# One product of the dense layers moved to the last place but one, and reads of banks and head statistics put ahead of weight splits

## The chip, the cores and the metric

The kernel runs on one core of a Trainium2 chip. Its engines are the matrix engine (PE, with PEld for its weight loads), the vector engine (DVE), the scalar engine (ACT), GpSimd (POOL) and SyncE (SP), which here only issues transfers. The metric is the device time of one execution in microseconds, as the median of several runs. Before the change it is 1388.97 us (three runs, 1386.44 to 1390.92).

## The reference

Two pre-norm residual layers over 512 tokens of width 1024, in float32, each a token mixer and a dense squared-ReLU block, and a final norm.

```python
def chunked_spatial_gating(xn, w_in, b_in, v_norm_g, w_s, b_s, w_out):   # mixer of layer 0
    u, v = split(gelu(xn @ w_in + b_in)); v = rmsnorm(v, v_norm_g)
    s = causal mix of v over chunks of 128 tokens by w_s, plus b_s
    return (u * s) @ w_out

def retention(xn, w_in, head_norm_g, w_out):                             # mixer of layer 1
    q, k, v, g = split(xn @ w_in)          # 4 heads, 256 for q and k, 512 for v and g
    o = decayed causal attention of rotary(q), rotary(k), v
    o = rmsnorm(o, head_norm_g) per head * silu(g)
    return o @ w_out

def squared_relu_mlp(h, w1, w2):                                         # 1024 -> 4096 -> 1024
    a = relu(h @ w1)
    return (a * a) @ w2

for i in range(2):
    x = x + mixer_i(rmsnorm(x, norm_mix_g[i]))
    x = x + squared_relu_mlp(rmsnorm(x, norm_ffn_g[i]), mlp_w1[i], mlp_w2[i])
return rmsnorm(x, final_norm_g)
```

## The kernel before, in words

**Splits.** Every float32 operand of a matmul is split into a high part, a cast to fp32r on ACT, and a low part, the operand less its high part, on DVE. A product is then three matmuls (`mm3`): high by high, high by low, low by high. Weights come in 1 MB tiles ("raw", one DMA each on SP's queue). A tile is used as two pieces; a piece gets its high part `wH` at L220 and its low part `wL` at L227.

**Order.** The kernel is a list of steps, written out by hand, and each engine works its instructions off in the order in which the steps emit them. A step is one piece of weights (24 matmuls for an up step or an output step, 12 for half a product of the kind below). Within a step `advance()` emits the next part of pending work (evacuations, activations), and `refill()` emits the weight work ahead: the casts up to the third piece after the step's own place, the low parts one piece less far. When all pieces of a tile are split, its slot is free and the next load is emitted; loads are emitted in the order of first use.

**The dense layers.** The up product makes 4096 features, 1024 at a time (`up` steps, eight pieces to a quarter). The down product of the first three quarters (q = 0, 1, 2: I call them thirds) is done by `seven`, a scheme with seven block products in place of eight: activations are kept as two blocks of features by two halves of tokens, and each of the products s = 0 to 6 multiplies one block, or a sum of blocks, with one weight block or a sum of weight blocks. `make(s)` forms and splits the activations of a product (sums on DVE at L748 to L755, cast at L763, low part at L764). Sums of weights are formed in memory: a second DMA, on POOL's queue (L199), adds a block onto the tile. The products 1, 3 and 6 share one tile: 3's weights are made by adding a block onto 1's once both pieces of 1 are split, 6's by adding onto 3's.

Each product accumulates into one of three pairs of PSUM banks, `BANK = "acbacaa"` by s, named smLQa, smLQb and smLQc in the profile (L the layer, Q the third); the bank of 0, 1 and 2 is opened there and later products add to what it holds. At the end of a product its bank is read into the token-major sum `ytok` or `xtok` (two instructions on DVE at L792, in the third 0 also on ACT). In the third 2 the steps stand as `upupupupuupuupp`: u is an up step, p a product, so that the last two products follow each other directly. After the last quarter's activations are ready, `split_a` splits them (L713, L714) for the last down product.

**The head statistics.** In layer 1, `o_unit` multiplies one head's gated output with its rows of the output weights, in four pieces (`ro`), and during it the norm of the next head is made by the generator `head_norm`: the sum of squares is split (ACT L316, POOL L317), summed over partitions by two matmuls (`st_h`, L325 and L326), scaled and put through a reciprocal square root on DVE (L329 to L303), split and laid on a diagonal (`dg_h`, L340), and spread over partitions by two matmuls (`bc_h`, L344 and L345). `out_piece` runs one piece: for each of two halves twelve matmuls, and in the second half `advance()`, `refill()` and then what the caller passes as `behind`.

Of the kernel before, what the change touches and what calls it, by code (L numbers as in the profile page):

```python
# [88 lines left out]
def trunk(ctx, tc, x, norm_mix_g, norm_ffn_g, a_w_in, a_b_in, a_v_norm_g, a_w_s, a_b_s, a_w_out,  # L89
# [16 lines left out]
    def tmp(name, tag, bufs=2):  # L106
        return work.tile([P, T], F32, tag=tag, name=name, bufs=bufs)
# [99 lines left out]
    def prep(upto, low=None):  # L207

        low = upto if low is None else low
        while pos["piece"] < min(upto, len(order)):  # L210
            p = order[pos["piece"]]
            if p.over is not None:
                lower(order.index(p.over) + 1)
            while any(raws.index(r) >= pos["raw"] for r in p.raws):
                load_raws()
                if any(raws.index(r) >= pos["raw"] for r in p.raws):
                    lower(pos["low"] + 1)
            prep_tiles(pos["piece"])
            p.src = p.make() if p.make else p.raws[0].tile[p.view]
            nc.scalar.copy(out=p.hi, in_=p.src)  # L220
            pos["piece"] += 1
        lower(low)
# [14 lines left out]
    def advance():  # L237
        for g in list(pending):
            if next(g, "end") == "end":
                pending.remove(g)  # L240
# [5 lines left out]
    def refill():  # L246
        n = pos["done"]
        prep(n + (LOOK if n >= 4 else 1), n + (LOOK - 1 if n >= 4 else 1))

    def step(fn, *ps):  # L250
        for p in ps:
            order.append(p)
            raws.extend(r for r in p.raws if r not in raws)
            for r in p.raws:
                r.uses += 1
        steps.append((fn, ps))
# [104 lines left out]
    def mm_o(p, t, ps, bH, bL):  # L361
        ts = slice(t * P, (t + 1) * P)
        for k in range(4):
            mm3(ps, p.hi[:, k, ts], p.lo[:, k, ts], bH[:, k, :], bL[:, k, :], k == 0, k == 3)
# [187 lines left out]
    def evac_x(gcol=None, scaled=False):  # L552

        def ev(i, ps):
            if scaled:
                t = tmp(f"xs{i}", "uz")
                nc.vector.tensor_mul(t, ps, r2bc)
                nc.vector.tensor_add(xT[i], xT[i], t)
            else:
                nc.vector.tensor_add(xT[i], xT[i], ps)  # L560
            if gcol is not None:
                norm_chunk(i, gcol)
        return ev

    def out_piece(p, i, h, name, gcol=None, before=None, behind=None, act=None, bank=acc, scaled=False):

        ev = evac_x(gcol, scaled)
        hi, lo = act or (yH, yL)

        def run(p):  # L570
            if before:
                before()
            for t in range(2):
                ps = bank(f"{name}{h}_{i}{t}")
                mm_o(p, t, ps, hi[h], lo[h])
                if t == 1:
                    advance()
                    refill()
                    if behind:
                        behind()  # L580
                ev(2 * i + t, ps)
        step(run, p)

    def nxt(g, times=1):
        return lambda: [next(g, None) for _ in range(times)]
# [133 lines left out]
    def seven(l, q):  # L719

        w = mlp_w2[l]

        def part(i, j):
            r, c = 1024 * q + 512 * i, 512 * j
            return w[r : r + 512, c : c + 512].rearrange("(k p) n -> p k n", p=P)

        t1 = Raw(part(0, 0), adds=[part(0, 1)])
        t2 = Raw(part(1, 1), adds=[part(1, 1)], over=t1)
        t4 = Raw(part(1, 0), adds=[part(1, 0)], over=t2)
        wraws = [Raw(part(0, 0)), t1, Raw(part(1, 0)), t2, Raw(part(1, 1)), Raw(part(0, 1), adds=[part(1, 1)]), t4]  # L730
        pl = [[Piece(r, (slice(None), slice(2 * i, 2 * i + 2), slice(None)), [P, 2, 512]) for i in range(2)] for r in wraws]
        lo_t, hi_t = slice(0, T // 2), slice(T // 2, T)
        sums, parts, banks = {}, {}, {}

        def block(h, ts, c):
            return aF[2 * q + h][:, 2 * c : 2 * c + 2, ts]

        def half(v):
            return v.rearrange("p (k t) -> p k t", t=T // 2)

        def make(s):

            def src(c):
                if s in (0, 2, 6):
                    return block(*((0, lo_t), None, (1, lo_t), None, None, None, (1, hi_t))[s], c)
                if s == 1:
                    sums["s", c] = half(tmp(f"sa{l}{q}{c}", "uz"))
                    nc.vector.tensor_sub(out=sums["s", c], in0=block(0, hi_t, c), in1=block(1, hi_t, c))  # L748
                elif s == 3:
                    nc.vector.tensor_sub(out=sums["s", c], in0=sums["s", c], in1=block(0, lo_t, c))  # L750
                elif s == 4:
                    nc.vector.tensor_add(out=sums["s", c], in0=sums["s", c], in1=block(1, lo_t, c))
                else:
                    sums["d", c] = half(tmp(f"sd{l}{q}{c}", "sq"))
                    nc.vector.tensor_sub(out=sums["d", c], in0=block(0, lo_t, c), in1=block(0, hi_t, c))  # L755
                    return sums["d", c]
                return sums["s", c]

            sp = parts[s] = big([P, 2, 4, T // 2], F32R, f"sp{l}{q}{s}")
            for c in range(2):  # L760
                v = src(c)
                hi, lo = sp[:, 0, 2 * c : 2 * c + 2, :], sp[:, 1, 2 * c : 2 * c + 2, :]
                nc.scalar.copy(out=hi, in_=v)  # L763
                nc.vector.tensor_sub(out=lo, in0=v, in1=f32(hi))  # L764

        BANK = "acbacaa"
        FIRST = (0, 1, 2)
        OUT = [((0, 0), ALU.add), ((1, 1), ALU.add), ((0, 0), ALU.add), ((0, 1), ALU.subtract), ((0, 1), ALU.add), ((1, 1), ALU.subtract), ((1, 0), ALU.add)]

        def one(s, i):  # L770
            def run(p):
                bk = BANK[s]
                if i == 0 and s in FIRST:
                    banks[bk] = [acc(f"sm{l}{q}{bk}{t}") for t in range(2)]
                sp = parts[s]
                for t in range(2):
                    ts = slice(t * P, (t + 1) * P)
                    for k in range(2):
                        kk = 2 * i + k
                        mm3(banks[bk][t], sp[:, 0, kk, ts], sp[:, 1, kk, ts], p.hi[:, k, :], p.lo[:, k, :], s in FIRST and kk == 0, kk == 3, True)  # L780
                advance()
                refill()
                if i == 0 and s < 6:
                    make(s + 1)
                if i == 1:
                    (m, n), op = OUT[s]
                    for t in range(2):
                        v = tok[n][:, 2 * m + t, :]
                        if (n, m) in fresh:
                            nc.scalar.activation(v, banks[bk][t], AF.Copy, scale=1.0 if op == ALU.add else -1.0)  # L790
                        else:
                            nc.vector.tensor_tensor(out=v, in0=v, in1=banks[bk][t], op=op)  # L792
                    fresh.discard((n, m))
            return run

        return (lambda: make(0)), [lambda s=s: [step(one(s, i), pl[s][i]) for i in range(2)] for s in range(7)]

    fresh = set()

# [167 lines left out]
    def make_y(h, cs):  # L967
        if 0 in cs:
            yH[h] = big([P, 4, T], F32R, f"ryH{h}")
            yL[h] = big([P, 4, T], F32R, f"ryL{h}")  # L970

        def gen():
            for c in cs:
                nc.vector.tensor_mul(oo[h][:, c, :], oo[h][:, c, :], r2bc)
                nc.scalar.copy(out=yH[h][:, c, :], in_=oo[h][:, c, :])
            for c in cs:
                nc.vector.tensor_sub(out=yL[h][:, c, :], in0=oo[h][:, c, :], in1=f32(yH[h][:, c, :]))
            return
            yield
        launch(gen())  # L980
# [20 lines left out]
    def o_unit(h, gcol=None, behind=None):  # L1001
        behind = behind or {}
        pl = pieces_o(b_w_out[0], (h * DV, (h + 1) * DV), (0, D))
        for i in range(4):
            out_piece(pl[i], i, h, "ro", gcol, behind=behind.get(i))

    def each(fn, h):
        return {i: (lambda i=i: fn(h, i)) for i in range(4)}

    def finish_head(h):  # L1010
        g = head_norm(h)
        return {0: nxt(g, 3), 1: nxt(g), 2: lambda: make_y(h, (0, 1)), 3: lambda: make_y(h, (2, 3))}

    v_unit(0, {0: nxt(nrm1), 1: nxt(nrm1, 2), 3: nxt(nrm1)})
    do(trig_scaled)
# [123 lines left out]
    for k in range(2):  # L1139
        p = order[0]  # L1140
# [52 lines left out]
```

## Time and profile before

| | |
|---|---|
| median of three runs | 1388.97 us (1386.44 to 1390.92) |
| the profiled execution | 1390.09 us, span 1388.4 us, mean granted clock 0.994 |
| PE busy | 1367.0 us (98% of the span), 6180 matmuls |
| PEld busy | 1134.7 us (82%) |
| DVE busy | 878.3 us (63%) |
| ACT busy | 567.8 us (41%) |
| POOL busy | 158.0 us (11%) |
| HBM read | 163.62 MB, 119 GB/s over the span |

All stages run under PE: the gating mixer to about 291 us, the dense layer 0 to 633, retention to 1036, the dense layer 1 to 1370, and the last rows to the end. The times in the profile's rows are microseconds from the start of the span. In rows of the timeline the first number is the start, the second the duration (of all instructions of the row, where xN stands at its end), and brackets give the idle time before it and what ended it. The rows of the page and of the trace on which the prediction rests stand in it.

### The profile page before, as it was taken

The numbers are of one execution on the slowest core, as the hardware profiler recorded it, in microseconds if no ns is written. First come the engines' busy times: TensorE is split into PE (matmuls) and PEld (weight loads), VectorE is DVE, ScalarE is ACT, GpSimd is POOL, SyncE is SP. The second block draws the span as 40 slices with busy tenths as digits, with TensorE's granted clock in tenths as the row PEclk, the third lists the DMA queues.
The fourth block names the chain that finished last, engine by engine and source line by source line (L and its number), as shares of the span: only waits on it lengthen the run. The fifth ranks groups of instructions, "written<-read, shape, count | busy, mean of one in ns | idle before, by whom it ended". The sixth has DMA issues, their size and how long they took to land.

```text
span 1388.4 us, 15488 instructions
## 1 busy us (share of the span) xinstructions
PE 1367.0 (98%) x6180; PEld 1134.7 (82%) x6180; DVE 878.3 (63%) x1228; ACT 567.8 (41%) x812; POOL 158.0 (11%) x122
## 2 busy tenths in 40 slices
PE   9999999999999999999999999999999999999997
PEld 7888888888888888788888888888888888888875
DVE  7757756666656766676656574574594576657555
ACT  4646634234544443422333332323334444444342
POOL 3010111130100100021111100100121000100002
PEclk9999999999999999999999999999999999999999
DMA  6332222245665754623222222131137475765611
GB/s 229 110 117 81 75 89 92 91 144 155 148 191 152 183 144 130 165 84 99 84 70 81 70 95 87 61 122 61 61 95 209 93 187 175 152 182 152 172 56 61
DMA packets 115801, 166.71 MB, mean 120 GB/s; under 512 B 2881, under 2 KB 67985, under 8 KB 115473
## 3 DMA queue, kind: packets, MB, share of 16 engines
q1 hardware_dynamic: 103024, 140.55, 30.5%
q0 software_dynamic: 12672, 25.17, 10.7%
q8 instruction: 48, 0.79, 0.2%
q14 instruction: 25, 0.20, 0.0%
q10 hardware_dynamic: 32, 0.01, 0.0%
HBM read 163.62 MB, written 2.10 MB: 119 GB/s over the span
## 4 chain that ended last, share of the span: by engine, by line
PE 95%; DVE 3%; POOL 0%; ACT 0%; issue 0%; DMA 0%; SPq 0%; ACTq 0%; DVEq 0%
PE up L264 24%; PE g L264 6%; PE vv L264 6%; PE qk L264 6%; PE u L264 6%; PE o L264 6%; PE v L264 5%; PE ro L264 5%; PE dt L264 3%; PE dn L264 2%; PE av L264 2%; PE sm11a L264 2%; PE sm10a L264 2%; PE sm01a L264 2%; PE sm00a L264 2%; PE sm02a L264 2%
## 5 line engine op out<-in xcount | busy, mean ns | idle before, releaser
L227 DVE TENSOR_TENSOR wL<-raw,wH 128x1024 fp32r<-128x1024 f32 x235 | 300.6, 1282 | 56.1 <-issue 17.9
L220 ACT CAST wH<-raw 128x1024 fp32r<-128x1024 f32 x235 | 244.4, 1046 | 87.5 <-PE dt L264 13.1
L264 PE MATMUL up<-hH,wH 128*128 128x512 f32 x480 | 187.2, 390 | 0.2 <-ACT xtok L1038 0.2
L264 PE MATMUL up<-hL,wH 128*128 128x512 f32 x480 | 186.8, 389 | 0.0
L264 PE MATMUL up<-hH,wL 128*128 128x512 f32 x480 | 186.8, 389 | 0.0
L696 ACT ACTIVATE aF<-r 128x512 f32<-128x512 f32 x54 | 34.2, 633 | 207.7 <-DVE r L695 207.7
L695 DVE SCALAR_TENSOR_TENSOR r<-up,wide 128x512 f32<-128x512 f32 x54 | 37.3, 691 | 126.3 <-PE up L264 117.8
L264 PEld LDWEIGHTS up<-hH,wH 128*128 128x128 f32 x480 | 90.1, 188 | 19.0 <-ACT xtok L1038 0.5
L264 PEld LDWEIGHTS up<-hH,wL 128*128 128x128 f32 x480 | 90.1, 188 | 18.9
L264 PEld LDWEIGHTS up<-hL,wH 128*128 128x128 f32 x480 | 90.1, 188 | 18.7
L199 POOL DMA_DIRECT2D raw<-in_mlp_w_dram x22 | 29.0, 1366 | 421.5 <-DVE wL L227 257.1
L293 POOL TENSOR_TENSOR ssq<-ssq,sq 128x512 f32<-128x512 f32 x28 | 43.0, 1536 | 149.9 <-ACT sq L292 149.6
L227 DVE TENSOR_TENSOR wL<-more,wH 128x1024 fp32r<-128x1024 f32 x40 | 48.7, 1218 | 7.9 <-issue 6.4
L264 PE MATMUL u<-hH,wH 128*128 128x512 f32 x128 | 50.6, 395 | 0.0
L264 PE MATMUL g<-hH,wH 128*128 128x512 f32 x128 | 50.5, 395 | 0.0
L264 PE MATMUL o<-yH,wH 128*128 128x512 f32 x128 | 50.4, 394 | 0.0
L220 ACT CAST wH<-more 128x1024 fp32r<-128x1024 f32 x40 | 41.9, 1047 | 20.7 <-PE sm02a L264 6.5
L264 PE MATMUL qk<-hH,wH 128*128 128x512 f32 x128 | 50.0, 391 | 0.0
L264 PE MATMUL vv<-wH,hH 128*128 128x512 f32 x128 | 50.0, 391 | 0.0
L264 PE MATMUL ro<-ryH,wH 128*128 128x512 f32 x128 | 50.0, 391 | 0.0
L264 PE MATMUL ro<-ryH,wL 128*128 128x512 f32 x128 | 49.9, 390 | 0.0
L264 PE MATMUL vv<-wL,hH 128*128 128x512 f32 x128 | 49.9, 390 | 0.0
(394 smaller groups left out, 3101.9 us busy)
## 6 DMA issues: line engine op xcount, KB each, us to landing
raw<-in_mlp_w_dram SPq DMA_DIRECT2D x50, 1024.0 KB, 5.2
raw<-in_b_w_in_dram SPq DMA_DIRECT2D x24, 1024.0 KB, 5.0
raw<-in_mlp_w_dram POOLq DMA_DIRECT2D x22, 1024.0 KB, 9.3
more<-in_mlp_w_dram SPq DMA_DIRECT2D x20, 1024.0 KB, 5.4
raw<-in_a_w_in_dram SPq DMA_DIRECT2D x14, 1024.0 KB, 5.1
raw<-in_a_w_out_dram SPq DMA_DIRECT2D x8, 1024.0 KB, 5.0
raw<-in_b_w_out_dram SPq DMA_DIRECT2D x8, 1024.0 KB, 4.9
raw<-in_a_w_in_dram SPq DMA_DIRECT2D x8, 256.0 KB, 6.1
```

The source lines that it names most:

```text
L199: nc.gpsimd.dma_start(out=r.tile, in_=src, accum_op=ALU.add)
L220: nc.scalar.copy(out=p.hi, in_=p.src)
L227: nc.vector.tensor_sub(out=p.lo, in0=p.src, in1=f32(p.hi))
L264: nc.tensor.matmul(ps, lhsT=a, rhs=b, start=start and i == 0, stop=stop and i == 2, skip_group_check=resumed)
L293: nc.gpsimd.tensor_tensor(out=state["ssq"], in0=state["ssq"], in1=sq, op=ALU.add)
L695: nc.vector.scalar_tensor_tensor(out=r, in0=ps, scalar=0.0, in1=rbc, op0=ALU.max, op1=ALU.mult)
L696: nc.scalar.activation(a, r, AF.Square)
```

## The change

Three things are changed.

First, in the third q = 2 of both dense layers the products are worked off in the order 0, 1, 3, 4, 5, 2, 6 instead of 0 to 6. Product 2 is the only one in bank pair b; it now stands between products 5 and 6, both in bank a. With it move its load, its splits and the activations that `make` forms.

Second, in every product the reads of the bank at its end are emitted ahead of `refill()` of that step instead of behind it.

Third, in the three `o_unit` calls with a `finish_head`, the first part of `head_norm` (the split of the sum of squares) is emitted ahead of the first piece's matmuls, and the second and third parts (statistics matmuls, root, diagonal) behind that piece's matmuls but ahead of `advance()` and `refill()`. Before, all three stood behind `refill()`.

```diff
-    def out_piece(p, i, h, name, gcol=None, before=None, behind=None, act=None, bank=acc, scaled=False):
+    def out_piece(p, i, h, name, gcol=None, before=None, early=None, behind=None, act=None, bank=acc, scaled=False):
...
                 if t == 1:
+                    if early:
+                        early()
                     advance()
                     refill()
                     if behind:
...
+        PLAN = (0, 1, 3, 4, 5, 2, 6) if q == 2 else range(7)
+
         def one(s, i):
+            after = dict(zip(PLAN, PLAN[1:])).get(s)
+
             def run(p):
...
                 advance()
-                refill()
-                if i == 0 and s < 6:
-                    make(s + 1)
+                if i == 0:
+                    refill()
+                if i == 0 and after is not None:
+                    make(after)
                 if i == 1:
                     (m, n), op = OUT[s]
...
                     fresh.discard((n, m))
+                    refill()
             return run
 
-        return (lambda: make(0)), [lambda s=s: [step(one(s, i), pl[s][i]) for i in range(2)] for s in range(7)]
+        return (lambda: make(0)), [lambda s=s: [step(one(s, i), pl[s][i]) for i in range(2)] for s in PLAN]
...
-            out_piece(pl[i], i, h, "ro", gcol, behind=behind.get(i))
+            out_piece(pl[i], i, h, "ro", gcol, before=behind.get((i, 0)), early=behind.get((i, 1)), behind=behind.get(i))
...
-        return {0: nxt(g, 3), 1: nxt(g), 2: lambda: make_y(h, (0, 1)), 3: lambda: make_y(h, (2, 3))}
+        return {(0, 0): nxt(g), (0, 1): nxt(g, 2), 1: nxt(g), 2: lambda: make_y(h, (0, 1)), 3: lambda: make_y(h, (2, 3))}
```

The order of instructions at three places follows; line numbers of the changed kernel are two to eight higher than those of the kernel before.

The first place is on ACT in layer 0, third 2, around the product that stands third. raw_3587 is the tile of the products 1, 3 and 6, raw_3765 that of product 2, more_2290 that of the up steps. Before:

```order
L696 ACTIVATE aF_0_3767<-r_3848 128x512
L220 CAST wH_3865<-raw_3765 128x1024
L763 CAST sp_3869<-aF_4_3507 128x512 x2
L220 CAST wH_3886<-raw_3765 128x1024
L220 CAST wH_3917<-more_2290 128x1024
```

And now:

```order
L698 ACTIVATE aF_0_3765<-r_3848 128x512
L220 CAST wH_3865<-raw_3587 128x1024
L765 CAST sp_3869<-sa_3788 128x512
L765 CAST sp_3869<-sa_3792 128x512
L220 CAST wH_3890<-raw_3587 128x1024
L220 CAST wH_3919<-more_2290 128x1024
```

The casts of the third product are now those of the shared tile, with the casts of its two sums (sa) between them.

The second place is on DVE at the end of the same third: the last two products. aL is from `split_a`. Before:

```order
L714 TENSOR_TENSOR aL_0_4225<-aF_0_3767,aH_0_4224 128x512 x4
L227 TENSOR_TENSOR wL_4216<-raw_3587,wH_4215 128x1024
L764 TENSOR_TENSOR sp_4250<-aF_4_3507,sp_4250 128x512 x2
L227 TENSOR_TENSOR wL_4247<-raw_3587,wH_4246 128x1024
L792 TENSOR_TENSOR ytok_2289<-ytok_2289,sm02a_3771 128x512
L792 TENSOR_TENSOR ytok_2289<-ytok_2289,sm02a_3772 128x512
```

And now:

```order
L716 TENSOR_TENSOR aL_0_4223<-aF_0_3765,aH_0_4222 128x512 x4
L227 TENSOR_TENSOR wL_4214<-raw_3587,wH_4213 128x1024
L766 TENSOR_TENSOR sp_4250<-aF_4_3507,sp_4250 128x512 x2
L799 TENSOR_TENSOR ytok_2288<-ytok_2288,sm02b_4232 128x512
L799 TENSOR_TENSOR ytok_2288<-ytok_2288,sm02b_4233 128x512
L227 TENSOR_TENSOR wL_4247<-raw_3587,wH_4246 128x1024
```

The reads are of bank b instead of a, and stand ahead of the low part of product 6's second piece.

The third place is on DVE in the first of the three heads, from the first read of a `ro` bank on; o and gt are the head's output and its gate, raw_5696 (raw_5695 now) is the tile of the third and fourth `ro` pieces. Before:

```order
L560 TENSOR_TENSOR xT_86<-xT_86,ro_00_5825 128x512
L960 TENSOR_TENSOR o_5644<-o_5644,gt_5661 128x512
L990 TENSOR_TENSOR gt_5661<-gz_5821,gs_5822 128x512
L227 TENSOR_TENSOR wL_5799<-raw_5696,wH_5798 128x1024
L329 TENSOR_TENSOR own_h_5865<-st_h_5862,ident 128x512
L330 TENSOR_REDUCE ms_h_5866<-own_h_5865 128x4
```

And now, with the thirteen small instructions between left out:

```order
L560 TENSOR_TENSOR xT_86<-xT_86,ro_00_5828 128x512
L329 TENSOR_TENSOR own_h_5858<-st_h_5855,ident 128x512
L330 TENSOR_REDUCE ms_h_5859<-own_h_5858 128x4
...
L340 TENSOR_TENSOR dg_h_5880<-ident,sp_h_0_5876 128x512
L340 TENSOR_TENSOR dg_h_5882<-ident,sp_h_1_5877 128x512
L968 TENSOR_TENSOR o_5643<-o_5643,gt_5660 128x512
L998 TENSOR_TENSOR gt_5660<-gz_5820,gs_5821 128x512
L227 TENSOR_TENSOR wL_5798<-raw_5695,wH_5797 128x1024
```

The two gating products and the low part of the third `ro` piece moved from ahead of the statistics to behind them.

## The prediction

> **What bounds the kernel now.** I read the page first, then what the matrix engine PE waited for, then the chain of waits, and then the places where PE stood still.
>
> ```profile
> PE 1367.0 (98%) x6180; PEld 1134.7 (82%) x6180; DVE 878.3 (63%) x1228; ACT 567.8 (41%) x812; POOL 158.0 (11%) x122
> PE 95%; DVE 3%; POOL 0%; ACT 0%; issue 0%; DMA 0%; SPq 0%; ACTq 0%; DVEq 0%
> ```
>
> PE is busy 98% of the span and carries 95% of the chain. No matmul is added or removed, so the change is worth what it adds to or takes from PE's pauses. The list of waits, PE alone:
>
> ```profile
> PE sm12a L264 <- DVE xtok L792: 3.2, 1, 3.2
> PE sm02a L264 <- DVE ytok L792: 3.2, 1, 3.2
> ...
> PE bc_h L344 <- DVE dg_h L340: 0.9, 3, 0.3
> PE st_mix L326 <- POOL st_mix L317: 0.9, 1, 0.9
> ```
>
> The largest two are the last product of the last third of each dense layer (sm02a in layer 0, sm12a in layer 1), which waits for the reads of the product before it out of the same bank. The three bc_h waits are the head statistics. The chain (start, duration, what) and a table by window (width; busy time of PE, PEld, DVE, ACT, POOL; granted clock; DMA share; GB/s) show what a long wait costs beyond itself:
>
> ```profile
> 558.65 10.88 PE up L264 x48
> 569.53 1.91 PE sm02a L264 x9
> 578.18 8.29 PE sm02a L264 x24
> 586.47 2.72 PE dn0a L264 x12
> ...
> 1318.60 1.91 PE sm12a L264 x9
> 1334.55 35.38 PE dt L264 x156
> ```
> ```profile
> 28.00:36.00 8.00, 7.02 (x30) 5.20 (x30) 4.95 (x11) 1.57 (x2) 3.55 (x3) 1.00 0.15 35
> 575.00:578.00 3.00, 0.00 (x0) 0.00 (x0) 3.00 (x6) 3.00 (x6) 0.00 (x0) 0.82 0.00 0
> 578.00:582.00 4.00, 3.82 (x9) 3.08 (x10) 4.00 (x7) 0.96 (x2) 0.00 (x0) 0.50 0.00 0
> 1327.00:1331.00 4.00, 3.75 (x10) 3.02 (x11) 4.00 (x7) 1.04 (x2) 0.00 (x0) 0.61 0.00 0
> ```
>
> Two steps of 24 matmuls take 10.88 us (first row), one takes 5.44. From 569.53 to 586.47 the last two products take 16.94 us, so 6.06 are lost; in layer 1, 1334.55 - 1318.60 = 15.95, 5.07 lost. The wait is 3.2 of each; the rest, 2.85 (8.29 - 5.44) and 1.86, is the granted clock at 0.50 and 0.61 behind it. The wait of 0.9 at about 32 us left the clock at 1.00.
>
> **The last product.** I call the seven products P0 to P6 by their table number and the halves of one a and b. What PE waited on, on VectorE (DVE):
>
> ```profile
> 573.88 1.22 DVE L227 TENSOR_TENSOR wL<-raw,wH 128x1024 fp32r<-128x1024 f32 x1
> 575.01 1.28 DVE L764 TENSOR_TENSOR sp<-aF,sp 128x512 fp32r<-128x512 f32 x2
> 576.22 1.22 DVE L227 TENSOR_TENSOR wL<-raw,wH 128x1024 fp32r<-128x1024 f32 x1
> 577.36 1.27 DVE L792 TENSOR_TENSOR ytok<-ytok,sm02a 128x512 f32<-128x512 f32 x2
> ```
>
> With P2 and its own bank in front of P6, P6 no longer waits for the reads at 577.36. What is late next is its own data. P6's first step would start at 574.97 (569.53 + 5.44). Its third matmul needs the low half of the activations, the first of the two instructions at 575.01, done at 575.65: with 0.15 to reach PE (the first read ended at 577.36 + 0.64 = 578.0, PE went on at 578.18), 575.8 instead of 575.4, 0.4 lost. Then DVE does the two reads (576.22 to 577.4) and only then the weight split of P6b, done at 578.65; that half's second matmul would be due at 578.3 and starts at 578.8, another 0.5. I take 1.0 us left per layer (if the third matmul waits for both instructions at 575.01 it loses 1.0 there and nothing after). Such a gap did not lower the clock at 32 us. Gain: (6.06 - 1.0) + (5.07 - 1.0) = **9.1 us**.
>
> **What P3 in third place costs.** P3's weights are built in P1's own tile: once P1b is split, POOL issues a DMA that adds a block onto it. Before, P2 and one up step lay between P1 and P3; now one up step does. On DVE, POOL, and ACT, with the time to landing of all such issues:
>
> ```profile
> 512.32 1.22 DVE L227 TENSOR_TENSOR wL<-raw,wH 128x1024 fp32r<-128x1024 f32 x1
> 513.84 1.28 POOL L199 DMA_DIRECT2D raw<-in_mlp_w_dram  x1 [29.00 <-DVE wL L227]
> 516.43 1.04 ACT L220 CAST wH<-raw 128x1024 fp32r<-128x1024 f32 x1
> 526.07 0.39 PE L264 MATMUL sm02b<-wL,sp 128*128 128x512 f32 x1
> DMA to landing us min/median/max: 8.4/9.0/17.5
> raw<-in_mlp_w_dram POOLq DMA_DIRECT2D x1, 1024.0 KB, 8.6
> ```
>
> P1b's split ends at 513.5 in both orders (the reads of P0 and P1a's split swap places in front of it, with the same sum), so the add leaves at 513.84 and lands 8.6 us later (last row, that one issue), at 522.4. The third product's cast, which ACT ran at 516.43 on P2's finished tile, is now P3a's and must wait for 522.4. Behind it on ACT stand the casts of P3's sums, and on DVE everything that needs them. How long that takes is read where P3 was made before (ACT's cast of the first sum, then DVE):
>
> ```profile
> 528.50 0.62 ACT L763 CAST sp<-sa 128x512 fp32r<-128x512 f32 x1 [0.16 <-DVE sa L750]
> 531.14 0.69 DVE L764 TENSOR_TENSOR sp<-sa,sp 128x512 fp32r<-128x512 f32 x1 [0.69 <-ACT sp L763]
> 531.74 1.22 DVE L227 TENSOR_TENSOR wL<-raw,wH 128x1024 fp32r<-128x1024 f32 x1
> 532.88 1.28 DVE L792 TENSOR_TENSOR ytok<-ytok,sm02b 128x512 f32<-128x512 f32 x2
> ```
>
> From the first cast (528.50) to the next free DVE slot (531.74) are 3.24 us. The reads of P1 now come first (1.2), then P3a's weight split (1.22): 5.7 behind that cast, which itself stands 1.0 (P3a's cast) behind the landing. So the split ends at 522.4 + 1.0 + 5.7 = 529.1 and PE's second matmul of P3a runs at 529.2. Before, the second matmul of the third product ran at 526.07. **Loss 3.1 us** in a layer, 6.2 in both: in layer 1 the same rows stand 749.07 us later (POOL at 1262.90, 12.24 before that matmul at 1275.14, as 513.84 before 526.07 is 12.23).
>
> ```profile
> 1262.90 1.28 POOL L199 DMA_DIRECT2D raw<-in_mlp_w_dram  x1 [28.95 <-DVE wL L227]
> 1275.14 0.39 PE L264 MATMUL sm12b<-wL,sp 128*128 128x512 f32 x1
> ```
>
> Bounds: 2.9 at a landing of 8.4 us, 3.5 at 9.0. And PE then stands still for 3.0 us, close to the 3.2 that halved the clock twice. I price that by the smaller of the two losses above, 1.86, since this wait is shorter: **3.7 us** for two layers (bounds 0 and 5.7).
>
> The other DMAs of that third: P5's load on SP takes a slot that comes free before P4's steps instead of behind them, and its add and P6's leave POOL one behind the other as before (the 17.5 us landing is of such a pair). Between that load and its use lie an up step, P4 and two more up steps, 21.8 us of PE. I cost it at nothing; if that cover were gone, ACT would wait for P5's tile as it does for P3's, another 3 us or so.
>
> **Reads ahead of weight splits elsewhere.** The split that now stands behind the reads is for the half after the next up step, 5.44 us of PE away, and the two reads take 1.28. That up step hides them; without it each product would lose up to 1.28. Nothing, in the thirds 0 and 1.
>
> **The head statistics** (three places alike; DVE, then PE, of the first):
>
> ```profile
> 792.36 0.69 DVE L560 TENSOR_TENSOR xT<-xT,ro 128x512 f32<-128x512 f32 x1 [3.95 <-PE ro L264]
> 795.22 1.21 DVE L227 TENSOR_TENSOR wL<-raw,wH 128x1024 fp32r<-128x1024 f32 x1
> 796.35 0.68 DVE L329 TENSOR_TENSOR own_h<-st_h,ident 128x512 f32<-128x512 f32 x1
> 800.48 1.29 DVE L340 TENSOR_TENSOR dg_h<-ident,sp_h 128x512 fp32r<-128x512 f32 x2
> 802.88 0.68 DVE L960 TENSOR_TENSOR o<-o,gt 128x512 f32<-128x512 f32 x1
> ```
> ```profile
> 795.12 0.40 PE L326 MATMUL st_h<-st_h,onesr 128*128 128x512 f32 x1
> 801.82 0.50 PE L345 MATMUL bc_h<-dg_h,onesr 128*128 128x512 f32 x1
> 802.60 0.39 PE L264 MATMUL ro<-ryH,wL 128*128 128x512 f32 x1
> ```
>
> The statistics matmul keeps its place on PE and ends at 795.52. Before, DVE used the time up to there for the head's gating product and the split at 795.22, then began the chain at 796.35. Now the chain stands first and DVE idles from 793.0 to 795.56; it gains 0.8 us and ends at 801.7 - 0.8 = 800.9, so bc_h no longer waits (some 0.85 us saved with its two slow matmuls). But the split of the third piece now stands behind the chain and two products: 800.9 + 0.6 + 0.6 (row of 802.88, 0.6 to the next) + 1.21 = 803.3. PE's third matmul of that piece needs it and ran at 802.60; now 803.45. **Loss 0.85 us**, three times: 2.5. Bounds: 0.85 gained if the split is in time after all; 1.65 lost if the chain starts no earlier than 796.35 did.
>
> **Sum.** Against the profiled execution's 1390.09 us (span 1388.4): -9.1 + 6.2 + 3.7 + 2.5 = +3.3, so 1393.4. That execution lies 1.1 above the median of 1388.97; for the median I forecast **1392.3 us**.
>
> **The rivals.**
>
> *The clock stays up at P3* (everything else alike). For it: the wait is shorter than the two that lowered the clock. Against: in 575 to 578 the mean is already 0.82 with PE idle, so the clock fell about 2 us into the wait. Time: +3.3 - 3.7 = -0.4, 1388.6. The Trainium skill, page "TensorE: Matmul & The Clock Gate", section "HAM oscillation — how this bites in real kernels", says that PE idle gaps above about 3.4 us are to be avoided, which would spare this 3.0 us gap; by that rule the 3.2 us waits here would have been spared too, and the trace shows that they were not.
>
> *P3 is hidden anyway* (faster). Then only the gain at P6 and the heads count: -9.1 + 2.5 = -6.6, 1382.4. It decides where the add lands within 5.5 us of its issue; the least in the trace is 8.4. Against it stands also ACT's order: P3a's cast is in front of everything that P3 needs.
>
> *The clock also falls at the heads* (slower). The third piece then stands still from about 802.0 to 803.45, 1.5 us; between 0.9 (clock kept) and 3.2 (clock lost) nothing in the trace decides, and the row of 575 to 578 puts the point near 2. It would add 1.86 at each of three heads: +3.3 + 5.6 = +8.9, 1397.9.
>
> *The head change does what it says*: no piece waits, bc_h is hidden, three times 0.85 gained: +3.3 - 2.5 - 2.5 = -1.7, 1387.3.
>
> **How the numbers follow.** About 0.3% (4.2 us) is what a measurement of this kernel can tell from no change. The forecast case has 0.52, and its own range is 1389.5 to 1396 (the bounds of P3's wait, 1.86 to 2.85 of clock, and 2 us about the median, as the three runs spread); 0.22 of it lies above 1393.2. Clock stays up 0.14, P3 hidden 0.12, clock falls at the heads 0.12, heads as meant 0.06; 0.04 is left for what would make it faster and I have not seen. Faster: 0.12 + 0.04 = 0.16. Slower: 0.22 + 0.12 = 0.34. The rest, 0.50, is no change. The range reaches from the hidden P3 to the slow heads: 1382 to 1399.
>
> **What would show it.** The list of PE's waits should have no sm02a or sm12a behind ytok or xtok, but a wait of about 3 us at the third product of the last third (new step of bank a, before 530 us and before 1280 us), ended by a weight split on DVE, and ACT waiting some 6 us for a DMA just before. The clock by windows shows below 1.00 there or not: that separates the first two cases. P6 should start within 1 us of the end of P2. At the heads, bc_h should not wait, and the third piece's third matmul should, for about 1.5 us, on a weight split. If ACT does not wait for the add, or the third piece finds its split done, the forecast is wrong there by the price given.

## The result, and the profile after

The changed kernel takes **1395.51 us** (median of five runs, 1393.36 to 1397.91) against 1388.97 us before (five runs beside it, 1386.44 to 1390.92): the ratio is 1.0053, with a 95% interval of 1.0034 to 1.0072. It is slower, by about 6.5 us; 1392.3 was forecast, with 1382 to 1399 as the range. The prediction drew the line between no change and slower at 4.2 us, so this is the slower kernel, to which it gave 0.34, and not the no change to which it gave 0.50. The profiled execution took 1397.42 us (span 1395.7, clock 0.995).

The busy times and the chain of waits by engine, from the page of the changed kernel:

```profile
PE 1368.7 (98%) x6180; PEld 1133.9 (81%) x6180; DVE 875.1 (63%) x1228; ACT 568.2 (41%) x812; POOL 158.0 (11%) x122
PE 86%; DVE 5%; issue 4%; DMA 3%; ACT 1%; POOL 0%; SPq 0%; ACTq 0%; POOLq 0%; DVEq 0%
```

PE's work is the same, but it now carries 86% of the chain where it carried 95%: the chain now also runs through DVE, a DMA and "issue", time in which the profile shows nothing that was waited for. The list of PE's waits (sum, times, longest):

```profile
PE ro L264 <- DVE wL L227: 4.1, 3, 1.4
PE sm02a L264 <- DVE wL L227: 3.0, 1, 3.0
PE sm12a L264 <- DVE wL L227: 2.8, 1, 2.8
PE xt L452 <- DMA xr<-in_x_dram: 2.7, 1, 2.7
...
PE dt L264 <- DVE wL L227: 0.5, 1, 0.5
PE dn0a L264 <- DVE wL L227: 0.3, 1, 0.3
```

The two waits for ytok and xtok are gone, and so are the three of bc_h. In their place stand a wait of 3.0 and 2.8 us for a weight split at the product that is now third, three of 1.4 us at the heads, and two short ones behind P6. The wait at the start (xt) was 1.0 us before; the change moves nothing there.

The chain in layer 0 shows where the wait at the third product comes from (start, duration, what):

```profile
516.38 8.68 DMA raw<-in_mlp_w_dram
525.16 1.05 ACT wH L220
526.21 0.53 ACT sp L765
...
529.43 1.19 DVE ytok L799 x2
530.62 1.15 DVE wL L227
531.82 7.10 PE sm02a L264 x23
...
577.00 1.91 PE sm02b L264 x9
...
586.01 2.49 DVE aL L716 x4
588.50 1.15 DVE wL L227
589.69 2.56 PE dn0a L264 x10
```

The add onto P1's tile, 8.68 us; P3a's cast on ACT; the casts of P3's sums; the reads of P1 (ytok); P3a's weight split; and only then PE. P2 (sm02b) now stands between P5 and P6. The last three rows are a second, smaller link, behind P6: dn0a's weight split stands behind the four low parts of the activations (aL).

The same from ACT and PE, with the idle time before each instruction in brackets:

```profile
525.16 1.05 ACT L220 CAST wH<-raw 128x1024 fp32r<-128x1024 f32 x1 [6.09 <-DMA raw<-in_mlp_w_dram]
531.82 0.50 PE L264 MATMUL sm02a<-wL,sp 128*128 128x512 f32 x1 [3.03 <-DVE wL L227]
806.44 0.50 PE L264 MATMUL ro<-ryH,wL 128*128 128x512 f32 x1 [1.37 <-DVE wL L227]
1283.97 0.79 PE L264 MATMUL sm12a<-wL,sp 128*128 128x512 f32 x1 [2.82 <-DVE wL L227]
```

The table by window behind the wait in layer 0; the granted clock is the third number from the end:

```profile
530.00:532.00 2.00, 0.18 (x1) 0.18 (x2) 2.00 (x4) 0.60 (x1) 0.00 (x0) 1.00 0.00 0
532.00:534.00 2.00, 2.00 (x7) 1.58 (x8) 2.00 (x3) 0.47 (x1) 0.00 (x0) 0.70 0.03 8
534.00:536.00 2.00, 2.00 (x6) 1.52 (x6) 1.31 (x3) 1.72 (x3) 0.00 (x0) 0.50 0.34 16
536.00:538.00 2.00, 2.00 (x10) 1.68 (x9) 1.31 (x3) 0.76 (x2) 0.00 (x0) 0.95 0.82 285
```

The clock fell to 0.50 and came back after 3.4 us: 0.30 x 2 + 0.50 x 2 + 0.05 x 2 = 1.7 us lost. It did the same behind the wait in layer 1, and it did not fall at the heads or behind P6.

**Where the 7.3 us between the two profiled executions went.** I compared the starts of the same matmuls in both (differences of starts, so waits and lowered clock together):

| part of the program | after - before, us |
|---|---|
| start-up, to the first matmul of u (the change moves nothing here) | +2.55 |
| the rest of mixer 0, and layer 0 up to its last third | 0.00 |
| last third of layer 0, and dn0a | +0.51 |
| three heads of retention | +2.79 |
| last third of layer 1, and dt | +1.38 |
| the parts that the change touches | **+4.68** |

### The profile page after: what moved, and what is told of

Read it like the earlier page. It is cut to its first block, busy times and chain, and to the rows that moved or that the text cites. A ratio compares the mean times of both kernels' runs of the same rounds, so it can differ in the third digit from the quotient of the medians.

```text
span 1395.7 us, 15453 instructions
## 1 busy us (share of the span) xinstructions
PE 1368.7 (98%) x6180; PEld 1133.9 (81%) x6180; DVE 875.1 (63%) x1228; ACT 568.2 (41%) x812; POOL 158.0 (11%) x122
## 4 chain that ended last, share of the span: by engine, by line
PE 86%; DVE 5%; issue 4%; DMA 3%; ACT 1%; POOL 0%; SPq 0%; ACTq 0%; POOLq 0%; DVEq 0%
PE up L264 19%; PE g L264 6%; PE vv L264 6%; PE qk L264 6%; PE u L264 6%; PE o L264 6%; PE ro L264 5%; PE v L264 5%; DMA raw<-in_mlp_w_dram 3%; PE dt L264 3%; PE dn L264 2%; PE av L264 2%; PE sm00a L264 2%; PE sm10a L264 2%; PE sm01a L264 1%
## 5 line engine op out<-in xcount | busy, mean ns | idle before, releaser
L227 DVE TENSOR_TENSOR wL<-raw,wH 128x1024 fp32r<-128x1024 f32 x231 | 290.2, 1268 | 51.5 <-issue 21.3
L220 ACT CAST wH<-raw 128x1024 fp32r<-128x1024 f32 x231 | 240.3, 1045 | 94.8 <-DMA raw<-in_mlp_w_dram 15.1
L227 DVE TENSOR_TENSOR wL<-more,wH 128x1024 fp32r<-128x1024 f32 x44 | 56.4, 1293 | 4.0 <-ACT wH L220 3.2
L220 ACT CAST wH<-more 128x1024 fp32r<-128x1024 f32 x44 | 45.8, 1047 | 10.8 <-PE dt L264 4.4
L264 PE MATMUL ro<-ryL,wH 128*128 128x512 f32 x128 | 50.0, 391 | 0.0
```

What stands on the lines that cost most here:

```text
L227: nc.vector.tensor_sub(out=p.lo, in0=p.src, in1=f32(p.hi))
L264: nc.tensor.matmul(ps, lhsT=a, rhs=b, start=start and i == 0, stop=stop and i == 2, skip_group_check=resumed)
```

## The experiments

Times are medians, with the kernel before run on the same chip beside each (1389.39 us in the first group, 1391.0 in the second).

### The three parts, one by one

**The order alone.** The kernel before, with the third q = 2 in the changed order, nothing else:

```diff
+        PLAN = (0, 1, 3, 4, 5, 2, 6) if q == 2 else range(7)
...
-                if i == 0 and s < 6:
-                    make(s + 1)
+                if i == 0 and after is not None:
+                    make(after)
...
-        return (lambda: make(0)), [lambda s=s: [...] for s in range(7)]
+        return (lambda: make(PLAN[0])), [lambda s=s: [...] for s in PLAN]
```

> The kernel before with one part of the change: the order of products 0, 1, 3, 4, 5, 2, 6 in the last third of each layer; refills (weight splits) stay ahead of the reads and the heads are untouched. My theory (P3's weights arrive late through the add-DMA behind P1b's split): P1's last reads now stand behind P3a's weight split on DVE, which comes 1.2 us earlier than in the changed kernel, so PE waits some 1.8 us at P3a instead of 3.0; P6 loses its bank wait of 3.2 us in each layer and keeps about 0.5 there, and a new wait of about 0.6 appears at the first matmuls behind P6 (dn0a, dt). If a 1.8 us wait leaves the clock up: 2 x (6.06 - 0.5) or 2 x (5.07 - 0.5) gained, about 10, against 2 x 1.9 for P3 and 2 x 0.6 behind P6, net -5, about 1384. If the clock drops there as it does in the changed kernel: 3.4 more, net -1.6, about 1387.5. Rival (P3's wait comes from the reads being ahead of its split, not from the DMA): no wait at P3a at all, -8 to -9, about 1380.

Measured: 1387.77 us, ratio 0.9988 (0.9979 to 0.9997). PE's waits at P3a, and the windows that follow them in layer 0 (first) and layer 1:

```profile
PE sm12a L264 <- DVE wL L227: 1.8, 1, 1.8
PE sm02a L264 <- DVE wL L227: 1.7, 1, 1.7
```
```profile
528.00:530.00 2.00, 2.00 (x9) 1.66 (x10) 2.00 (x3) 0.00 (x0) 0.00 (x0) 1.00 0.04 8
...
1276.00:1278.00 2.00, 2.00 (x7) 1.58 (x6) 2.00 (x3) 0.29 (x1) 0.00 (x0) 0.53 0.00 0
```

The rival falls: with the reads behind the split, P3a still waits, because ACT waits for the same add.

```profile
522.51 1.05 ACT L220 CAST wH<-raw 128x1024 fp32r<-128x1024 f32 x1 [5.95 <-DMA raw<-in_mlp_w_dram]
```

But two waits that differ by 0.1 us had opposite ends: the clock stayed at 1.00 after the one and fell to 0.50 after the other. That is followed up below. The median is the one expected for a clock that falls in both layers, but it fell in one; in this execution the first matmuls behind P6 (dn0a and dt) cost 1.1 and 1.3 us where 0.6 each was expected, so the agreement is in part luck.

**The heads alone.** The kernel before with the `before=`, `early=` and `finish_head` lines of the change:

```diff
-            out_piece(pl[i], i, h, "ro", gcol, behind=behind.get(i))
+            out_piece(pl[i], i, h, "ro", gcol, before=behind.get((i, 0)), early=behind.get((i, 1)), behind=behind.get(i))
...
-        return {0: nxt(g, 3), 1: nxt(g), 2: ...
+        return {(0, 0): nxt(g), (0, 1): nxt(g, 2), 1: nxt(g), 2: ...
```

> The kernel before with one part of the change: the statistics chain and gating products of a head ahead of the weight split of the third output piece. My theory: the third matmul of the third piece waits 1.4 us on the split at three heads and bc_h no longer waits; each head costs 0.9 us more, +2.8, about 1391.8; before the first head nothing moves. Rival (the heads' share seen between the two profiled executions is scatter and the chain that starts earlier pays): three times 0.85 gained, about 1386.4.

Measured: 1392.45 us, ratio 1.0018 (1.0010 to 1.0027). From its trace, the largest of PE's waits; then, from the trace of the changed kernel, DVE at the first head, which has the same order there:

```profile
PE ro L264 <- DVE wL L227: 4.1, 3, 1.4
```
```profile
798.62 0.69 DVE L329 TENSOR_TENSOR own_h<-st_h,ident 128x512 f32<-128x512 f32 x1 [2.52 <-PE st_h L326]
...
802.76 1.29 DVE L340 TENSOR_TENSOR dg_h<-ident,sp_h 128x512 fp32r<-128x512 f32 x2
...
...
805.17 1.22 DVE L227 TENSOR_TENSOR wL<-raw,wH 128x1024 fp32r<-128x1024 f32 x1
```

DVE idles 2.52 us for the statistics matmuls, a gap that held the weight split before, and the split ends at 806.4, 1.37 us too late. The three heads cost 2.82 us between this execution and the profiled one of before, 0.94 each; apart from the start-up (0.78 us) nothing else of the program is slower. The rival is out.

**The reads alone.** The kernel before with the reads of a finished bank ahead of `refill()`:

```diff
                 advance()
-                refill()
+                if i == 0:
+                    refill()
...
                     fresh.discard((n, m))
+                    refill()
```

> The kernel before with one part of the change: the reads of a finished pair of banks stand ahead of the refill of a weight split, in every third; the order of the products is as before. My theory: in thirds 0 and 1, and wherever an up step lies between, nothing is seen; before P6 the two reads that PE waits for come one weight split (1.2 us) earlier, so the wait of 3.2 falls to about 2.0 in both layers: -2.3, about 1386.7; if the clock then stays up at 2.0 us, another 1.9 to 2.9 a layer, down to about 1382. Rival (a split that is put off costs its product later): slower by up to 1.2 for each of some 40 products, visible as PE waits on weight splits; at +1 us or more the rival holds.

Measured: 1386.72 us, ratio 0.9972 (0.9960 to 0.9983).

```profile
PE sm02a L264 <- ACT aH L713: 2.1, 1, 2.1
PE sm12a L264 <- ACT aH L713: 2.1, 1, 2.1
...
576.40 1.27 DVE L793 TENSOR_TENSOR ytok<-ytok,sm02a 128x512 f32<-128x512 f32 x2
577.23 0.72 PE L264 MATMUL sm02a<-wH,sp 128*128 128x512 f32 x1 [2.08 <-ACT aH L713]
```

The wait before P6 is 1.1 us shorter in each layer. The row names ACT, but PE goes on 0.19 us after the first of the two reads (576.40 + 0.64 = 577.04), as it did before. In the first two thirds no start of a matmul moves by more than 0.03 us against the others of its layer: putting the split off is free there.

### What the third product waits for

**Order and reads together, without the heads.** Each of the two gained alone. The edit is the sum of the two diffs.

> The changed kernel with the heads as before: the order of products and the reads ahead of refills together. Alone, the order gained 1.6 us (its wait at P3a was 1.7 and 1.8 us) and the reads gained 2.7. My theory: together they undo each other, since P1's reads now stand ahead of P3a's split and the wait there is 3.0 again, long enough to lower the clock in both layers; from the profiled changed kernel the two thirds cost 0.5 + 1.4 = 1.9 against the profiled kernel before, so 1391 to 1392.5. Rival (the parts add up): -1.6 - 2.7, about 1385; then the changed kernel's loss would lie in the heads and the start-up.

Measured: 1392.2 us, ratio 1.0012 (1.0003 to 1.0020).

```profile
PE sm12a L264 <- DVE wL L227: 3.1, 1, 3.1
PE sm02a L264 <- DVE wL L227: 2.9, 1, 2.9
```
```profile
528.00:530.00 2.00, 0.55 (x1) 0.50 (x2) 2.00 (x3) 0.23 (x1) 0.00 (x0) 0.68 0.00 0
530.00:532.00 2.00, 2.00 (x6) 1.56 (x5) 2.00 (x3) 0.83 (x2) 0.00 (x0) 0.50 0.03 8
532.00:534.00 2.00, 2.00 (x6) 1.51 (x6) 1.31 (x3) 1.36 (x2) 0.00 (x0) 0.50 0.16 20
534.00:536.00 2.00, 2.00 (x7) 1.58 (x6) 1.31 (x3) 1.12 (x2) 0.00 (x0) 0.62 0.99 353
```

The parts don't add up (-1.6 and -2.7 make +1.2). With the heads, measured alone, this makes 1.0030 (1.0012 and 1.0018), against 1.0053 (1.0034 to 1.0072) for the whole change; the intervals meet, so no further interplay is shown. Each gains by shortening or removing the wait at P6, and that gain can be had only once; and at P3a the reads now stand ahead of the one split that is late, which brings that wait from 1.7 back to 2.9. Here the clock stayed at 0.50 for 6.8 us in both layers, twice as long as in the changed kernel after the same wait.

**P0 between P1 and P3.** P2 keeps its place between the last two products, but P1 goes first, so that P0 and an up step lie between P1 and P3. Heads and reads are as in the kernel before; against the order alone:

```diff
-        PLAN = (0, 1, 3, 4, 5, 2, 6) if q == 2 else range(7)
+        PLAN = (1, 0, 3, 4, 5, 2, 6) if q == 2 else range(7)
```

> The kernel before with the order 1, 0, 3, 4, 5, 2, 6 in the last third (refills and heads as before): P2 still stands between the last two of bank a, but P0 now lies between P1 and P3, so the add-DMA for P3's weights has the same lead as in the kernel before. My theory (P3's loss is the DMA's lead): no PE wait at P3, clock at 1.00 there, P6 keeps about 0.5, and some 0.6 behind P6: net 2 x (5.6 - 0.5) less 2 x 0.6, -8 to -9, about 1380.5. Rival (whatever stands third in that third waits, because the statistics of sums and reads are late on ACT and DVE): a wait of 2 to 3 us at P3 or P0 again, about 1388.

Measured: 1382.45 us, ratio 0.9949 (0.9935 to 0.9963). PE's waits in the two thirds, and the add on POOL:

```profile
PE dt L264 <- DVE wL L227: 1.0, 1, 1.0
...
PE dn0a L264 <- DVE wL L227: 0.8, 1, 0.8
...
504.13 1.28 POOL L199 DMA_DIRECT2D raw<-in_mlp_w_dram  x1 [27.16 <-DVE wL L227]
```

P3a's cast on ACT in layer 1:

```profile
1261.02 1.05 ACT L220 CAST wH<-raw 128x1024 fp32r<-128x1024 f32 x1 [0.88 <-DMA raw<-in_mlp_w_dram]
```

The add leaves some 9 us earlier than with the order alone (513.87, less 1.1 by which that execution was later), and PE waits nowhere in the third (dn0a and dt stand behind it); the clock stays at 1.00 to the last rows. The rival is out. The lead is only just long enough, though: the add took 11.2 us to land in layer 0 and 12.1 in layer 1, against 8.5 and 8.7 with the order alone (why was not tested), so that ACT idled 5.95 us for it with the order alone, not at all here in layer 0, and 0.88 in layer 1. The gain of 6.9 is smaller than expected: by the starts of matmuls P2 and P6 keep 0.6 a layer (0.5 expected), but dn0a and dt lose 1.05 and 1.31 with what follows their waits, where 0.6 each was expected.

**The same order in the changed kernel**, all else as changed:

```diff
-        PLAN = (0, 1, 3, 4, 5, 2, 6) if q == 2 else range(7)
+        PLAN = (1, 0, 3, 4, 5, 2, 6) if q == 2 else range(7)
...
-        return (lambda: make(0)), [...]
+        return (lambda: make(PLAN[0])), [...]
```

> The changed kernel with one thing different: in the last third the order is 1, 0, 3, 4, 5, 2, 6, so that P0 lies between P1 and P3 (reads and heads as in the changed kernel). My theory: the wait of 3.0 and 2.8 us at P3a and the 1.7 us of lowered clock behind each go away, 9.3 us in all, and P6 and what follows it keep the 0.3 and 0.5 waits of the changed kernel; with the heads' 2.8 still in it about 1384 to 1386. Rival (with the reads ahead of the splits the third product waits whatever the lead of the DMA): a wait of over 1 us at a weight split in that third remains, and the time stays above 1389.

Measured: 1386.26 us, ratio 0.9971 (0.9960 to 0.9981).

```profile
PE ro L264 <- DVE wL L227: 4.1, 3, 1.4
...
PE dt L264 <- DVE wL L227: 0.5, 1, 0.5
PE dn0a L264 <- DVE wL L227: 0.3, 1, 0.3
```

So the whole change turns from a loss into a gain by a trade of two products' places. The short lead of the add is shown to be the cause of the waits at P3; the reads ahead of the split only lengthen them.

**A better kernel.** The order 1, 0, 3, 4, 5, 2, 6, the reads ahead, the heads as before, and the last four activation splits behind P6, where they no longer stand ahead of dn0a's and dt's weight splits (the first two edits as shown above):

```diff
-                    if q == 2 and j == 6:
+                    if q == 2 and j == 7:
                         do(lambda: [split_a(l, i) for i in range(4, 8)])
```

> A version meant to be better: order 1, 0, 3, 4, 5, 2, 6, reads ahead of refills, heads as before, and the splits of the last four activation chunks moved behind P6, so that they no longer stand ahead of the weight splits of dn0a and dt. Against the order 1, 0, 3, 4, 5, 2, 6 alone (7 us faster than before), the waits of 0.8 (dn0a) and 1.0 (dt) should go: -8.5 to -9.3 against before, 1380 to 1381. Rival (what is moved only moves the wait): dn0a or dt then waits on the activation splits (aL or aH) by as much or more, 1382 or above.

Measured: **1382.05 us** (1381.61 to 1382.39) against 1391.0 before on that chip, ratio 0.9942 (0.9930 to 0.9953). Of PE's waits behind the start-up only those of bc_h and one of 0.2 us are left:

```profile
PE bc_h L344 <- DVE dg_h L340: 0.9, 3, 0.3
PE up L264 <- ACT xtok L1044: 0.2, 1, 0.2
```

The waits of dn0a and dt are gone and no wait on aL or aH came in their place, so the rival is out. The 9 us are within what was expected; the absolute time is not, as that chip ran the kernel before at 1391.0. That the two last edits gain over the order 1, 0, 3, 4, 5, 2, 6 alone is not shown by the medians: the intervals of the ratios (0.9930 to 0.9953 and 0.9935 to 0.9963) overlap. In the two traces, from the first matmul of u to the last ones of dt, they gain 1.0 us.

### When the clock falls

Waits of 1.7 and 1.8 us with opposite ends, and 3.4 or 6.8 us of lowered clock after waits of 3 us: the length of the wait alone does not decide. In each of the traces with more than one lowered stretch, all of them begin at one phase of a period of 3.413 us. In the changed kernel, from windows of 1 us (a window at 0.89 has 0.22 us at 0.50, so the stretch begins at 532.78; the other begins at 1283.72):

```profile
532.00:533.00 1.00, 1.00 (x5) 0.78 (x6) 1.00 (x2) 0.00 (x0) 0.00 (x0) 0.89 0.06 16
...
1283.00:1284.00 1.00, 0.03 (x1) 0.03 (x1) 1.00 (x2) 0.00 (x0) 0.00 (x0) 0.86 0.00 0
```

750.94 us lie between, 220.0 periods. So I measured pauses by themselves.

> All of the computation is left out and the output is zeros: PE runs bursts of 36 to 48 matmuls of the same form (8 to 11 us), 90 pauses between them are set by one to five DVE copies (about 0.5 to 3.8 us in ten steps, each nine times at other points of time), then 12 pairs of pauses of some 0.9 us with three matmuls (0.7 us) between them. Theory A (from six traces of this case, in each of which every lowered stretch begins at one phase of a period of 3.41 us): the clock is judged in fixed stretches of 3.41 us, and the next is run at 0.50 when PE stood still for more than about 1.75 us in one; pauses up to 1.7 never lower it, pauses of 1.8 to 3.4 do or don't by where they lie (2.0: spared some 4 of 9 times, 3.0: 1 or 2 of 9), pauses above 3.5 always do, and some of the pairs lower it although neither pause is above 1.0. Theory B (the length of one pause decides, at about 2 us as the prediction put it): every pause above one length lowers the clock and none below, wherever it lies, and no pair does. Theory C (only a pause of a whole 3.4 us counts): none of the pauses below 3.4 lowers it.

> As the run with pauses alone, computation left out and the output not written beyond zeros: PE bursts of 36 to 48 matmuls with pauses of about 1.8, 1.9, 2.0, 2.6, 3.0, 3.5, 3.9 and 5.2 us, nine of each, and 18 pairs of pauses of 1.1 us with three matmuls (0.7 us) between them. The first such run lowered the clock after every stretch of 3.41 us with 1.96 us or more of PE idle and after none with 1.89 or less, wherever the pause lay. Open was whether idle time in one stretch adds up. Theory A1 (the sum in the stretch counts): a pair, 2.2 us of idle in 2.9, lowers the clock when the stretch holds over 1.9 of it, that is in some 5 of 18. Theory A2 (the longest single pause in a stretch counts): no pair does. For both: pauses of 2.6 lower it in about 5 of 9, of 3.0 in 7 of 9, of 3.5 and more in 9 of 9. Second question, how long it stays low: in the kernels of this case it stayed low for a second stretch when that one still held 0.72 us of idle or more, and not at 0.46 or less; the pauses of 3.0 to 5.2 should show that bound again, at stretches of 6.8 us and more against 3.41.

In both, PE runs bursts of `matmul(ps, lhsT=eyeR, rhs=...)`, and a pause is a chain of DVE copies of which the first reads the burst's bank and the last writes what the next burst's first matmul reads. The pauses of the first run came out shorter than planned (0.3 to 2.6 us; its pairs, 24 pauses of 0.78, add up to 1.56 each), so that its pairs told nothing, and the second run was made for that. All pauses of both runs:

| pause, us | count | clock fell after | of these for two stretches |
|---|---|---|---|
| 0.3 to 1.7 | 96 | 0 | 0 |
| 1.94 to 2.13 | 36 | 21 | 0 |
| 2.49 to 2.63 | 18 | 9 | 0 |
| 3.09 | 9 | 8 | 1 |
| 3.55 | 9 | 7 | 2 |
| 4.01 | 9 | 9 | 7 |
| 5.40 | 9 | 9 | 6 |
| pair of 1.11 and 1.11, 0.7 apart | 18 | 7 | 0 |

Two pauses of the same length, one lowered and one spared, from the second run, with the window behind each:

```profile
160.03 0.50 PE L170 MATMUL ps<-rhs,eyeR 128*128 128x512 f32 x1 [2.63 <-DVE rhs L176]
...
626.23 0.50 PE L170 MATMUL ps<-rhs,eyeR 128*128 128x512 f32 x1 [2.63 <-DVE rhs L176]
```
```profile
162.00:164.00 2.00, 2.00 (x6) 1.52 (x5) 0.00 (x0) 0.00 (x0) 0.00 (x0) 0.50 0.00 0
...
628.00:630.00 2.00, 2.00 (x10) 1.64 (x9) 0.00 (x0) 0.00 (x0) 0.00 (x0) 1.00 0.00 0
```

Cut by the fixed stretches of 3.413 us, the outcomes of single pauses fall apart cleanly. Of the stretches at full clock, one with 1.94 us or more of PE idle was followed by one at 0.50 in every case of both runs; one with 1.89 or less in a single pause never was; of three between, one was. The pause of 157.40 to 160.03 lies whole in one stretch; that of 623.60 to 626.23 is cut in two by a border. Idle time adds up within a stretch: seven pairs lowered the clock, at sums of 1.67 to 2.22, though no single pause was above 1.11, so theory A2 falls. Theory B falls with the two pauses of 2.63, and theory C with those of 1.94 to 2.63 that lowered the clock. The plain sum is not the whole rule either: two pairs lowered the clock at sums of 1.67 and 1.72, where single pauses of up to 1.89 did not; why is open. A stretch at 0.50 was followed by another when it held 0.68 us of idle or more (16 of 16), and by full clock at 0.55 or less. The expectation that every pause of 3.5 lowers the clock was wrong: a border in its middle leaves two parts of 1.8, and two of nine were spared.

The kernels fit, with the border a little lower than for the single pauses. Idle in the stretch before, from the traces of the nine kernels behind the start-up: 1.38 (heads) and 1.70 spared; 1.81, 1.96, 2.07, 2.08, 2.18, 2.35, 2.45, 2.57, 2.76, 2.80, 2.96 lowered; a second stretch at 0.72 to 1.25 us of idle, none at 0.46 or less. In the start-up the border is less sharp (1.79 lowered, 1.95 spared).

## Why the prediction was right, and where its sizes were off

The forecast case came about: the gain at P6 is eaten by P3, its clock, and the heads. Its size did not: the forecast was 3.3 us over the median before, and 6.5 were measured. By its steps, from the traces:

- **P6, gain 9.1.** P2 and P6 together take 11.93 and 11.95 us in the changed kernel against 10.88 of matmuls: 1.05 and 1.07 left, where 1.0 was taken. The gain against the profiled execution before is 9.0. The size of what is gained against is chance, though: that execution lost 2.85 us to the clock in layer 0, two stretches. In the trace of the heads alone the same wait of 3.21 us was followed by one stretch, and that layer was 1.2 us faster.
- **P3, loss 6.2.** Measured 3.03 + 2.82 = 5.85. The steps are in the rows: the add lands 8.68 us after its issue (8.6 taken), ACT waits 6.09 ("some 6"), the reads go ahead of the split.
- **Clock after P3, 3.7.** It fell once in each layer: 1.71 + 1.70 = 3.4. The bounds 0 and 5.7 were right as bounds, the reason was wrong: the prediction read "about 2 us into the wait" out of the profile, as if the wait's length alone decided. It is the idle time that falls into one stretch of a fixed grid, so the wait's place counts as well. Of nine pauses of 3.09 us one cost nothing, seven one stretch and one two; "the clock stays up", put at 0.14, had about that chance at each of the two waits, which is far less for both, and not by the rule that the prediction tried. That each layer lost one stretch was luck, too: with order and reads together, the same waits cost two in each layer.
- **What the prediction did not have:** the wait behind P6. With P6 on time, dn0a and dt need their weight splits earlier, and these stand behind the four low parts of the activations: +0.61 and +0.82 us (starts of dn0a's and dt's later matmuls against their first ones), 1.4 in all. The rows that it would have taken were those of aL on DVE in front of the first dn split: the stall at P6 had been the cover, and the prediction followed what is late next only as far as P6b.
- **Heads, 2.5.** Measured 2.79 and 2.82. The wait is 1.37 (about 1.5 forecast), bc_h does not wait, and the clock stays up. The rival by which it falls there is out: in 96 pauses of up to 1.7 us it never did.
- **Reads ahead elsewhere, nothing; P5's load, nothing.** Both right: the first two thirds do not move, and PE's list has no wait at P5.
- **The sum.** Forecast +3.3 against the profiled execution, measured +4.68 in the parts that the change touches. Of the difference of 1.4 the waits of dn0a and dt explain +1.4, the heads +0.3, and P3 with its clock -0.6; the rest, +0.3, was not traced further.

The median is 3.2 us above the forecast, and the parts leave 1.8 of that open. Three things of that size vary from run to run. The start-up, the same instructions in all kernels, ended between 1.0 us earlier and 2.5 us later than in the profiled execution before, in nine traces; 2.5 is the changed kernel's. The kernel before loses one or two stretches at each P6, by chance. And the changed kernel loses one or more at each P3: one in its trace, two behind the same waits in that of order and reads; the mean granted clocks of its five runs lie between 0.993 and 0.997.

The chance in the kernel before shows in the granted clock that stands beside each run. Of its 41 runs in the two groups of experiments, the 14 at 0.996 took 1386.1 to 1389.0 us, and the 27 at 0.993 or 0.994 took 1389.3 to 1392.5. One stretch lowers the mean by 0.0012 (1.71 of 1388 us), so the groups lie about two stretches apart; that these fell at P6 is not on record for the runs without a trace. The chance can be seen in the spread, too: 18 runs of the kernel before lie within 5.7 us and 12 of order and reads within 4.8; the kernel with the good order and the changed heads, in which no wait behind the start-up is over 1.4 us, within 0.5 (seven runs), and the better kernel within 0.8 (six). Against it, the kernel with the good order and nothing else spread over 2.9 (five runs) with no such wait, so chance has other ways too. How much of the 1.8 each has was not settled, since only one execution of each kernel has a trace.

## What to carry to other kernels

When a stall goes, follow the engine's list to the next instruction that the stall had covered, and then to the one behind that: here P6, then dn0a. Before a step is moved, look at what its operands are made of, and count the lead of each DMA in steps: a tile that is added onto in place can only be begun when its last user is done with it. Two edits that take the same wait away don't add up, and one can lengthen the wait that the other makes.

## What was not expected of the hardware

PE's clock is judged in fixed stretches of 3.413 us, and the next runs at 0.50 when PE stood still for long enough in one: in one pause, 1.94 us always did in the runs of pauses and 1.89 never, and in the kernels 1.81 did and 1.70 did not; in two pauses, 1.67 was enough. A stretch at 0.50 costs 1.7 us of matmul time (half of 3.413). A single pause of up to 1.7 us never lowered it, one of 2.0 did 21 times in 36, and one of 3.55 was spared twice in nine, by its place alone. The Trainium skill, page "TensorE: Matmul & The Clock Gate", section "What's actually happening", has the free-running window of 3413 ns, which the traces agree with (220.0 periods between two stretches of one run). It has the clock lowered after a whole idle window, and there the runs differ: 1.94 us of idle in one were enough. So a wait between 1.8 and about 3.8 us (twice 1.9, cut by a border in its middle; an estimate) has no fixed price. The runs of the kernel before, with two waits of 3.2 us, fall into two groups some 3 us apart, and the granted clock parts them in the same way.
